# The first unit of weights multiplied for both tiles of tokens by row blocks, with its loads cut into pieces on two DMA queues

## The chip, the cores and the metric

The kernel runs on one core of a Trainium2 chip. The metric is the time of the whole launch on that core in microseconds: 2056.93 us is the median of three runs (2055.18 to 2057.09). Engines are named as the profile names them: PE (TensorE matmul) and PEld (its weight loads), DVE (VectorE), ACT (ScalarE), POOL (GpSimd), SP (SyncE, which here only issues DMAs). Each engine works through its own instructions in the order in which they were built.

## The reference, cut to what matters

A decoder trunk of four layers over 256 tokens of width 1024. Layer i is

```
x += 1/2 SwiGLU(rmsnorm x);  x += W_out [mixer heads | memory heads];  x += 1/2 SwiGLU(rmsnorm x)
swiglu(x) = (silu(x @ wg) * (x @ wu)) @ wd          # wg, wu: 1024 x 2816, wd: 2816 x 1024
rms_norm(x, g) = x * rsqrt(mean(x * x) + EPS) * g
```

with retention, indexed sparse attention, native sparse attention and again retention as the mixers of the four layers. Four heads of every layer attend to 256 memory tokens, which are normed by `rms_norm(mem)` first. All of it is float32. The change is in the first SwiGLU of the first layer: its first 256 gate and 256 up columns.

## The kernel before, in words

**Tiles and units.** The 256 tokens are two tiles of 128 (t = 0 and 1, `X[0]` and `X[1]`, 128 x 1024 each). All weights are streamed once, as units: a unit of kind "g" is 1024 rows x 512 columns (256 gate, 256 up), stored as two halves (`raw`, 128 x 2048 each, 1 MB; four row blocks of 128 rows each). There are three `raw` buffers. Both tiles use a unit before the next one comes.

**Products in three parts.** A float32 product is made of three matmuls (`mm3`, L231 to L235): high part x high part, high x low, low x high. So every quarter of a unit (two row blocks, 128 x 1024) is split: `hi` on ACT (L205) and `lo` = raw - hi on DVE (L206). The activations are split too: `norm_half` (L319) transposes four 128 x 128 blocks of `X` on PE (L329, into the bank `pT`), and makes `sh` on ACT (L333) and `sl` on DVE (L334), a block at a time, with the gain of the norm. A unit for one tile is 8 row blocks x 3 = 24 matmuls (`project`, L237) into one PSUM bank `pg`, of which there are two.

**What follows a unit.** For a unit of kind "g", ACT makes `th` (tanh, L1072), DVE `th` again (L1073) and `h` (L1075), which empties the bank; PE transposes `h` (L1081). `rh` and `r2` in these come from the token's norm: ACT squares a whole tile of `X` (`scr`, L341), and POOL makes `rstd_m`, `rstd`, `rh`, `r` of the sum (L314, L316, L344, L346).

**The memory's tokens.** `memory()` (L1178) loads two blocks `memx` of 512 KB on POOL's queue (L1184), and ACT squares them (L1186). On POOL these loads stand behind the norm of the first tile.

**The order.** The program is written by generators, one chain for each tile (`chain`, L1111) and one for the memory; a `tick` (L251) issues the steps that are due, one or two splits, and steps of a joint queue, whose number in a tick follows from a count of ticks (`JRATE`). A scheduler then fixes the order of each engine's instructions. At the start `run` (L1140) loads the identity, `X[0]` and the gains, then unit 0 in four pieces of 512 KB, then `X[1]` and unit 1, all on SP's queue; the constants `cf`, `cb`, `mqk` are written further down, on POOL's queue. Nine matmuls on zeros (`warm`) run on PE meanwhile.

## Time and profile before

| | |
|---|---|
| launch, median of 3 runs | 2056.93 us |
| span of the profiled execution, first to last instruction | 2052.0 us |
| median minus span (what lies around the span) | 4.9 us |
| PE busy | 2034.5 us, 99% of the span |
| PEld busy | 1652.5 us, 81% |
| DVE busy | 1257.3 us, 61% |
| ACT busy | 1025.5 us, 50% |
| POOL busy | 165.6 us, 8% |
| HBM read | 349.07 MB, 171 GB/s over the span |

A line of the timeline begins with the start and the length of an instruction (or of a run of like ones, xN) in us from the start of the span; what stands in brackets is the time the engine was idle before it, and what ended that. Neighbouring instructions of an engine overlap a little in the record, so the step from one start to the next is what an instruction costs in a queue; the length is what the last one of a chain costs. "Granted clock" is PEclk in tenths or hundredths of full speed: 1.00 is 2.4 GHz, 0.50 is 1.2 GHz.

### The profile page before, as it was taken

How to read it: one execution, taken by the hardware profiler on the slowest of the kernel's cores; microseconds unless marked ns; L12 is line 12 of the kernel's file. 1: busy time of each engine (PE TensorE's matmuls, PEld its weight loads, DVE VectorE, ACT ScalarE, POOL GpSimd, SP SyncE). 2: the span in 40 equal slices, each digit the busy share in tenths (PEclk: the TensorE clock that was granted, in tenths of full speed). 3: DMA queues.
4: the chain of work that ended last, by engine and by line, in shares of the span. 5: the costliest groups of instructions: out<-in, count | busy, mean ns of one | idle time of the engine just before them, and what ended most of it. 6: DMA issues, size and time to landing. Idle time of an engine off the chain costs nothing.

```text
span 2052.0 us, 25183 instructions
## 1 busy us (share of the span) xinstructions
PE 2034.5 (99%) x9658; PEld 1652.5 (81%) x9658; DVE 1257.3 (61%) x1996; ACT 1025.5 (50%) x1581; POOL 165.6 (8%) x290
## 2 busy tenths in 40 slices
PE   9999999999999999999999999999999999999999
PEld 6888777888888887888888878878888888778887
DVE  6555756555655687755665576665656656657553
ACT  6445555444544555544544455554445444546442
POOL 1000411000000122000000013220000000300000
PEclk9999999999999999999999999999999999999999
DMA  8454525445445423545445453134545545435452
GB/s 301 182 191 164 198 109 205 180 180 195 179 170 202 164 99 123 205 164 205 173 176 205 169 178 134 63 133 176 205 164 185 198 172 204 146 122 187 183 190 77
DMA packets 50153, 351.75 MB, mean 171 GB/s; under 512 B 5648, under 2 KB 5936, under 8 KB 9200
## 3 DMA queue, kind: packets, MB, share of 16 engines
q1 hardware_dynamic: 48816, 347.15, 46.3%
q0 software_dynamic: 640, 1.94, 0.3%
q8 instruction: 76, 1.25, 0.2%
q10 hardware_dynamic: 576, 1.05, 0.1%
q14 instruction: 45, 0.37, 0.1%
HBM read 349.07 MB, written 1.05 MB: 171 GB/s over the span
## 4 chain that ended last, share of the span: by engine, by line
PE 96%; DVE 2%; POOL 1%; ACT 1%; issue 0%; DMA 0%; SPq 0%; ACTq 0%; DVEq 0%; POOLq 0%
PE pg L235 16%; PE pg L233 16%; PE pg L234 16%; PE acc L233 8%; PE acc L234 8%; PE acc L235 8%; PE p L233 3%; PE p L235 3%; PE p L234 3%; PE pT L1081 2%; PE po L233 1%; PE po L234 1%; PE po L235 1%; PE pT L379 1%; PE pT L329 1%; PE nsa_s L429 1%
## 5 line engine op out<-in xcount | busy, mean ns | idle before, releaser
L206 DVE TENSOR_TENSOR lo<-raw,hi 128x1024 fp32r<-128x1024 f32 (+2 forms) x648 | 780.1, 1220 | 368.6 <-ACT hi L205 353.2
L205 ACT ACTIVATE hi<-raw 128x1024 fp32r<-128x1024 f32 (+2 forms) x648 | 667.3, 1049 | 373.0 <-PE acc L235 208.6
L233 PE MATMUL pg<-hi,sh 128*128 128x512 f32 x1408 | 563.2, 400 | 3.4 <-ACT hi L205 3.4
L235 PE MATMUL pg<-hi,sl 128*128 128x512 f32 x1408 | 552.0, 392 | 0.0
L234 PE MATMUL pg<-lo,sh 128*128 128x512 f32 x1408 | 550.1, 391 | 0.5 <-DVE lo L206 0.5
L235 PEld LDWEIGHTS pg<-hi,sl 128*128 128x128 f32 x1408 | 264.7, 188 | 57.6 <-DVE sl L334 0.3
L233 PEld LDWEIGHTS pg<-hi,sh 128*128 128x128 f32 x1408 | 265.0, 188 | 54.5 <-ACT hi L205 3.6
L234 PEld LDWEIGHTS pg<-lo,sh 128*128 128x128 f32 x1408 | 265.5, 189 | 52.8 <-DVE lo L206 1.0
L233 PE MATMUL acc<-hi,hT 128*128 128x512 f32 x704 | 281.2, 399 | 0.0
L234 PE MATMUL acc<-lo,hT 128*128 128x512 f32 x704 | 279.2, 397 | 0.0
L235 PE MATMUL acc<-hi,hT 128*128 128x512 f32 x704 | 277.5, 394 | 0.0
L1072 ACT ACTIVATE th<-pg,rh 128x256 f32<-128x256 f32 x176 | 83.6, 475 | 262.3 <-PE pg L235 262.3
L1073 DVE SCALAR_TENSOR_TENSOR th<-th,pg 128x256 f32<-128x256 f32 x176 | 73.5, 418 | 194.1 <-ACT th L1072 194.1
L235 PEld LDWEIGHTS acc<-hi,hT 128*128 128x128 f32 x704 | 132.3, 188 | 30.5 <-DVE hT L1083 0.2
L233 PEld LDWEIGHTS acc<-hi,hT 128*128 128x128 f32 x704 | 132.3, 188 | 30.1 <-ACT hT L1082 1.2
L234 PEld LDWEIGHTS acc<-lo,hT 128*128 128x128 f32 x704 | 132.5, 188 | 28.1
L1082 ACT ACTIVATE hT<-pT 128x256 fp32r<-128x256 f32 x176 | 65.9, 374 | 131.9 <-PE pT L1081 131.9
L233 PE MATMUL p<-hi,sh 128*128 128x512 f32 (+4 forms) x320 | 125.4, 392 | 0.0
L235 PE MATMUL p<-hi,sl 128*128 128x512 f32 (+4 forms) x320 | 120.9, 378 | 0.0
L234 PE MATMUL p<-lo,sh 128*128 128x512 f32 (+4 forms) x320 | 120.8, 377 | 0.0
L1083 DVE TENSOR_TENSOR hT<-pT,hT 128x256 fp32r<-128x256 f32 x176 | 74.1, 421 | 37.3 <-ACT hT L1082 37.2
L333 ACT ACTIVATE sh<-pT,gains 128x128 fp32r<-128x128 f32 x192 | 63.5, 364 | 59.1 <-PE pT L329 39.6
(287 smaller groups left out, 1793.1 us busy)
## 6 DMA issues: line engine op xcount, KB each, us to landing
raw<-gu SPq DMA_DIRECT2D x174, 1024.0 KB, 4.8
raw<-dn SPq DMA_DIRECT2D x88, 1024.0 KB, 4.8
raw<-ret SPq DMA_DIRECT2D x20, 1024.0 KB, 4.8
raw<-wout SPq DMA_DIRECT2D x16, 1024.0 KB, 4.8
raw<-mkv SPq DMA_DIRECT2D x8, 1024.0 KB, 4.9
raw<-nsa SPq DMA_DIRECT2D x6, 1024.0 KB, 4.8
raw<-memT SPq DMA_DIRECT2D x4, 1024.0 KB, 4.8
raw<-dsa SPq DMA_DIRECT2D x4, 768.0 KB, 4.3
```

The source lines that it names most:

```text
L205: nc.scalar.activation(hi, src, AF.Copy)
L206: nc.vector.tensor_sub(lo, src, hi.bitcast(F32))
L233: mm(out, ah, bh, start=start, stop=False)
L234: mm(out, ah, bl, start=False, stop=False)
L235: mm(out, al, bh, start=False, stop=stop)
L329: nc.tensor.transpose(p[:, k], self.X[t][:, c * 128:(c + 1) * 128], self.ident)
L333: nc.scalar.activation(hi[:, c], p[:, k], AF.Copy, scale=gain)
L1072: nc.scalar.activation(th, p[:, :256], AF.Tanh, scale=rh)
L1073: nc.vector.scalar_tensor_tensor(th, th, 1.0, p[:, :256], op0=OP.add, op1=OP.mult)
L1081: nc.tensor.transpose(c[:, k], h[:, k * 128:k * 128 + 128], self.ident)
L1082: nc.scalar.activation(hl[:, 0], c[:, :2], AF.Copy)
L1083: nc.vector.tensor_sub(hl[:, 1], c[:, :2], hl[:, 0].bitcast(F32))
```

## The change

Unit 0 is no longer taken by `project`. A new function `opening` loads, splits and multiplies it for both tiles, and returns the two banks, which `ffn` then uses. The loads of `X` and of unit 0's first half become pieces of 256 KB, those of its second half pieces of 512 KB; `ident`, `gains` and three of the four pieces of `X` go out on ACT's queue. Three of the four half-norms are made by `norm_wide`, with instructions of 512 columns. The squares for the norm's factors (`norm_stats`) are written after the matmuls of unit 0. Four more matmuls on zeros stand before the first real one. The call that loads the constants is written behind the sixth step of the main loop. Comments and docstrings go as well, which moves the line numbers.

```diff
+    def norm_wide(self, t, g, b, st):
+        hi, lo = st["s"]
+        p = self.pC("pT")
+        c = slice(4 * b, 4 * b + 4)
+        for k in range(4):
+            nc.tensor.transpose(p[:, k], self.X[t][:, (4 * b + k) * 128:(4 * b + k + 1) * 128], self.ident)
+        w = self.t2([128, 4, 128], "xg")
+        nc.vector.tensor_mul(w, p, self.gains[:, g, c, None].to_broadcast([128, 4, 128]))
+        nc.scalar.activation(hi[:, c], w, AF.Copy)
+        nc.vector.tensor_sub(lo[:, c], w, hi[:, c].bitcast(F32))
...
             if kind == "g":
-                p = self.pB("pg")
-                self.project(p, s, u)
+                if u == 0:
+                    p = self.first[t]
+                else:
+                    p = self.pB("pg")
+                    self.project(p, s, u)
...
+    def opening(self):
...
+        nc.sync.dma_start(self.X[0][:, col(0)], x[0:128, col(0)])
+        nc.scalar.dma_start(self.ident, a["ident"])
+        nc.sync.dma_start(raw[0][:, col(0)], w[0][:, col(0)])
+        nc.scalar.dma_start(self.gains.rearrange("p a b -> p (a b)"), a["gains"])
+        nc.scalar.dma_start(self.X[1][:, col(0)], x[128:256, col(0)])
+        nc.sync.dma_start(raw[0][:, col(1)], w[0][:, col(1)])
+        nc.scalar.dma_start(self.X[0][:, col(1)], x[0:128, col(1)])
+        nc.sync.dma_start(raw[0][:, col(2)], w[0][:, col(2)])
+        nc.scalar.dma_start(self.X[1][:, col(1)], x[128:256, col(1)])
+        nc.sync.dma_start(raw[0][:, col(3)], w[0][:, col(3)])
+        for b in range(2):
+            c = slice(1024 * b, 1024 * b + 1024)
+            nc.sync.dma_start(raw[1][:, c], w[1][:, c])
+        self.fetch()
...
+        self.norm_half(0, g, 0, self.st[0])
+        halve(0, 1)
+        self.idle(4)
+        multiply(0, 0)
...
+        self.norm_wide(1, g, 0, self.st[1])
+        halve(1, 1)
+        multiply(0, 1)
+        multiply(1, 0)
+        multiply(1, 1)
+        self.norm_wide(0, g, 1, self.st[0])
+        halve(2, 1)
+        multiply(0, 2)
+        multiply(1, 2)
+        self.norm_wide(1, g, 1, self.st[1])
+        halve(3, 1)
+        multiply(0, 3)
+        multiply(1, 3)
+        for k in (4, 6):
+            halve(k, 2)
+            for t, j in ((0, 0), (1, 0), (0, 1), (1, 1)):
+                multiply(t, k + j)
+        for t in range(2):
+            self.norm_stats(t, self.st[t])
+        return p
...
-        for b in range(2):
-            self.norm_half(t, 2 * self.layers[0], b, st)
-        if t:
-            for x in range(2):
-                self.norm_stats(x, self.st[x])
...
-        nc.gpsimd.dma_start(self.cf, a["cf"])
-        nc.gpsimd.dma_start(self.cb, a["cb"])
...
+            if n == 5:
+                constants_in()
```

`halve(k, n)` is the split of n row blocks from the k-th (L1163 on ACT, L1164 on DVE), `multiply(t, k)` the three matmuls of row block k for tile t.

Three places show how the engines' orders move. The first is ACT, around the first `th`. Before, with the norm's blocks (L333), the splits of unit 1 (L205), `th` of tile 0 (L1072) and the squares of the memory's tokens (L1186):

```order
L205 ACTIVATE hi<-raw 128x1024 [waits DMAHW0_49]
L333 ACTIVATE sh_148<-pT,gains 128x128 [waits DVE_49] x2
L205 ACTIVATE hi<-raw 128x1024
L1072 ACTIVATE th<-pg,rh 128x256 [waits PE_49,Pool_49]
L333 ACTIVATE sh_148<-pT,gains 128x128 [waits DVE_49] x2
L205 ACTIVATE hi<-raw 128x1024 [waits DMAHW1_49]
L205 ACTIVATE hi<-raw 128x1024
L1186 ACTIVATE memx,memss<-memx 128x1024 [waits DMASW3_49]
L1186 ACTIVATE memx,memss<-memx 128x1024 [waits DMASW4_49]
L1082 ACTIVATE hT<-pT 128x256 [waits PE_49]
```

And in the changed kernel (L1163 splits unit 0, L349 squares `X`, L200 splits unit 1, L1252 squares `memx`, L1083 is `th`):

```order
L1163 ACTIVATE hi<-raw 128x1024 [waits DMAHW3_49]
L349 ACTIVATE scr,ss<-x_70 128x1024 [waits DMAHW6_49]
L342 ACTIVATE sh_136<-xg 128x512 [waits DVE_49]
L349 ACTIVATE scr,ss<-x_71 128x1024 [waits DMAHW4_49,DMAHW0_49]
L200 ACTIVATE hi<-raw 128x1024 [waits DMAHW4_49]
L200 ACTIVATE hi<-raw 128x1024
L1252 ACTIVATE memx,memss<-memx 128x1024 [waits DMASW3_49]
L200 ACTIVATE hi<-raw 128x1024 [waits DMAHW5_49]
L1083 ACTIVATE th<-pg,rh 128x256 [waits PE_49,Pool_49]
L200 ACTIVATE hi<-raw 128x1024
L1252 ACTIVATE memx,memss<-memx 128x1024 [waits DMASW4_49]
```

The square of `X[0]`, the second instruction of ACT before, now stands behind the splits of unit 0, and the first `th` behind a square of `memx`, which waits for its load.

The second place is PE, where unit 0 ends and unit 1 begins. Before (sh_148 and sl_149 are tile 1's operand, sh_104 tile 0's; L1081 transposes `h` of tile 0):

```order
L235 MATMUL pg<-hi,sl_149 128x512
L233 MATMUL pg<-hi,sh_148 128x512 [waits Activation_49]
L1081 MATMUL pT<-ident,h 128x128 [waits DVE_49]
L1081 MATMUL pT<-ident,h 128x128
L234 MATMUL pg<-lo,sh_148 128x512
L235 MATMUL pg<-hi,sl_149 128x512
L233 MATMUL pg<-hi,sh_104 128x512 [waits PE_49]
```

And changed (sh_110 is tile 0's operand, sh_136 tile 1's; L1092 transposes `h`):

```order
L230 MATMUL pg<-hi,sl_111 128x512
L228 MATMUL pg<-hi,sh_136 128x512
L229 MATMUL pg<-lo,sh_136 128x512
L230 MATMUL pg<-hi,sl_137 128x512
L1092 MATMUL pT<-ident,h 128x128 [waits DVE_49]
L1092 MATMUL pT<-ident,h 128x128
L228 MATMUL pg<-hi,sh_110 128x512 [waits PE_49,Activation_49]
```

The transposes of tile 0's `h` stood 22 matmuls behind tile 0's last matmul, and now stand three behind it, ahead of all of unit 1.

The third is POOL, in the changed kernel, from its first DMA (L1240 to L1242 are the constants, L1250 the memory's tokens):

```order
L1240 DMA cf<-cf 128x657
L1241 DMA cb<-cb 128x542
L1242 DMA mqk<-mqk 128x8
L1246 ISA
L1246 TENSOR_TENSOR mqkp<-mqk 128x4 [waits DMASW2_49]
L309 TENSOR_SCALAR rstd_m<-ss 128x1 [waits Activation_49]
L311 TENSOR_TENSOR rstd<-rstd_m,neghalf 128x1 [waits DVE_49,Pool_49]
L352 TENSOR_SCALAR rh<-rstd 128x1 [waits Pool_49]
L354 TENSOR_TENSOR r_235<-rstd 128x1
L1250 DMA memx<-mem 128x1024
L309 TENSOR_SCALAR rstd_m<-ss 128x1 [waits Activation_49]
L1250 DMA memx<-mem 128x1024
```

Here nothing moved: before, the same twelve stand in the same order with the same waits, the constants first. Elsewhere the orders differ only in the native sparse attention of the third layer, where steps of the two tiles stand a few rows earlier or later, since two ticks fewer were counted.

## Rows read from the trace of the kernel before

**Rows 1.** The page, busy time of each engine in the whole span.

```profile
PE 2034.5 (99%) x9658; PEld 1652.5 (81%) x9658; DVE 1257.3 (61%) x1996; ACT 1025.5 (50%) x1581; POOL 165.6 (8%) x290
```

**Rows 2.** Busy time by stretches of the opening: stretch, its length, then busy us (and instructions) of PE, PEld, DVE, ACT, POOL, then granted clock, DMA share, GB/s.

```profile
0.00:5.00 5.00, 3.82 (x10) 1.23 (x10) 0.29 (x2) 1.41 (x2) 2.06 (x7) 1.00 0.56 186
5.00:10.00 5.00, 1.63 (x10) 1.39 (x9) 0.83 (x3) 2.98 (x7) 0.92 (x3) 0.94 1.01 332
10.00:15.00 5.00, 4.54 (x10) 3.25 (x11) 5.00 (x10) 5.00 (x10) 1.82 (x4) 0.50 1.03 424
15.00:20.00 5.00, 5.00 (x25) 4.11 (x25) 3.35 (x6) 3.64 (x10) 2.27 (x5) 0.88 1.01 417
20.00:25.00 5.00, 5.00 (x23) 3.87 (x22) 5.00 (x10) 5.00 (x9) 0.57 (x1) 1.00 0.90 346
25.00:30.00 5.00, 5.00 (x25) 4.16 (x24) 4.20 (x7) 4.89 (x8) 1.86 (x4) 1.00 0.88 308
```

**Rows 3.** PE in the timeline of the opening: the first transposes, the first two matmuls, two more of unit 0 that follow each other, the transposes of tile 0's `h`, the matmul behind them, and the first matmul of unit 1 (25.62).

```profile
5.00 1.53 PE L329 MATMUL pT<-ident,x 128*128 128x128 f32 x8
9.89 0.79 PE L233 MATMUL pg<-hi,sh 128*128 128x512 f32 x1 [3.37 <-ACT hi L205]
11.15 0.80 PE L234 MATMUL pg<-lo,sh 128*128 128x512 f32 x1 [0.47 <-DVE lo L206]
13.02 0.63 PE L235 MATMUL pg<-hi,sl 128*128 128x512 f32 x1
13.45 0.63 PE L233 MATMUL pg<-hi,sh 128*128 128x512 f32 x1
24.94 0.38 PE L1081 MATMUL pT<-ident,h 128*128 128x128 f32 x2
25.07 0.48 PE L234 MATMUL pg<-lo,sh 128*128 128x512 f32 x1
25.62 0.40 PE L233 MATMUL pg<-hi,sh 128*128 128x512 f32 x1
```

**Rows 4.** Stretches of 0.2 us around the fall and the rise of the granted clock (columns as in rows 2).

```profile
9.20:9.40 0.20, 0.00 (x0) 0.00 (x0) 0.00 (x0) 0.20 (x1) 0.18 (x1) 0.96 0.90 369
9.40:9.60 0.20, 0.00 (x0) 0.00 (x0) 0.00 (x0) 0.20 (x1) 0.13 (x1) 0.50 0.98 389
16.20:16.40 0.20, 0.20 (x4) 0.20 (x3) 0.00 (x0) 0.00 (x0) 0.20 (x1) 0.97 1.60 655
```

**Rows 5.** ACT in the timeline of the opening.

```profile
4.87 1.06 ACT L341 ACTIVATE scr<-x 128x1024 f32<-128x1024 f32 x1 [2.86 <-DMA x<-x]
8.78 1.06 ACT L205 ACTIVATE hi<-raw 128x1024 fp32r<-128x1024 f32 x1 [1.85 <-DMA raw<-gu]
14.14 1.07 ACT L341 ACTIVATE scr<-x 128x1024 f32<-128x1024 f32 x1
15.09 0.22 ACT L341 ACTIVATION_READ_ACCUMULATOR scr<-x 128x1 f32 x1
20.42 0.48 ACT L1072 ACTIVATE th<-pg,rh 128x256 f32<-128x256 f32 x1
20.78 0.64 ACT L333 ACTIVATE sh<-pT,gains 128x128 fp32r<-128x128 f32 x2
23.17 1.08 ACT L1186 ACTIVATE memx<-memx 128x1024 f32<-128x1024 f32 x1
24.21 1.08 ACT L1186 ACTIVATE memx<-memx 128x1024 f32<-128x1024 f32 x1
26.94 2.96 ACT L205 ACTIVATE hi<-raw 128x1024 fp32r<-128x1024 f32 x3
```

**Rows 6.** DVE in the same timeline: splits (L206), blocks of the norm (L334), `h`; and a line of 128x512 from the end of the kernel.

```profile
9.87 1.22 DVE L206 TENSOR_TENSOR lo<-raw,hi 128x1024 fp32r<-128x1024 f32 x1 [2.56 <-ACT hi L205]
11.01 0.60 DVE L334 SCALAR_TENSOR_TENSOR sl<-pT,gains,sh 128x128 fp32r<-128x128 f32 x2
22.75 1.22 DVE L206 TENSOR_TENSOR lo<-raw,hi 128x1024 fp32r<-128x1024 f32 x1
23.89 0.47 DVE L1075 SCALAR_TENSOR_TENSOR h<-th,r,pg 128x256 f32<-128x256 f32 x1
2042.75 0.69 DVE L1100 SCALAR_TENSOR_TENSOR x<-acc,x 128x512 f32<-128x512 f32 x1 [2.10 <-PE acc L235]
```

**Rows 7.** POOL in the same timeline: the norm of tile 0, and the first load of the memory's tokens.

```profile
9.19 0.19 POOL L314 TENSOR_SCALAR rstd_m<-ss 128x1 f32<-128x1 f32 x1
11.29 0.62 POOL L1184 DMA_DIRECT2D memx<-mem  x1
```

**Rows 8.** DMA issues, KB each and us from issue to landing: the two loads of `memx` (issued at 11.29 and 16.16), the constants `cf`, and `X[1]` (issued at 4.13), each from the stretch in which it ran.

```profile
memx<-mem POOLq DMA_DIRECT2D x1, 512.0 KB, 7.8
memx<-mem POOLq DMA_DIRECT2D x1, 512.0 KB, 7.6
cf<-cf POOLq DMA_DIRECT2D x1, 328.5 KB, 4.6
x<-x SPq DMA_DIRECT2D x1, 512.0 KB, 9.6
```

**Rows 9.** Two stretches of the third layer's native sparse attention (columns as in rows 2).

```profile
1240.00:1300.00 60.00, 58.93 (x387) 51.25 (x385) 35.32 (x88) 30.89 (x65) 16.11 (x25) 1.00 0.32 116
1300.00:1350.00 50.00, 49.59 (x311) 39.77 (x311) 33.25 (x83) 27.64 (x56) 15.71 (x21) 1.00 0.28 105
```

More of the change, by code (lines that the diff above doesn't have):

```diff
@@ L181, in fetch @@
             r = self.wp.tile([128, n], F32, name="raw", tag="raw", bufs=3)
-            if u == 0:
-                for b in range(2):
-                    c = slice(b * n // 2, (b + 1) * n // 2)
-                    self.nc.sync.dma_start(r[:, c], ap[:, c])
-            else:
-                self.nc.sync.dma_start(r, ap)
+            self.nc.sync.dma_start(r, ap)
             self.raw[u].append(r)
@@ L335, in norm_half @@
                                            op0=OP.mult, op1=OP.subtract)
+    def norm_wide(self, t, g, b, st):
+        nc = self.nc
+        hi, lo = st["s"]
[7 more added lines that the diff above has]
+        nc.vector.tensor_sub(lo[:, c], w, hi[:, c].bitcast(F32))
     def norm_stats(self, t, st):
@@ L1109, in ffn, with idle, halve, multiply @@
             self.norm_stats(t, st)
+    def idle(self, n):
+        for _ in range(n):
+            self.nc.tensor.matmul(self.pw, self.warm[:, :128], self.warm, start=True, stop=True)
+    def opening(self):
+        nc, a, g = self.nc, self.a, 2 * self.layers[0]
+        x, w = a["x"], self.units[0][1]
+        self.n_fetch = self.n_split = 1
+        raw = [self.wp.tile([128, 2048], F32, name="raw", tag="raw", bufs=3) for _ in range(2)]
+        col = lambda k: slice(512 * k, 512 * k + 512)
+        nc.sync.dma_start(self.X[0][:, col(0)], x[0:128, col(0)])
[12 more added lines that the diff above has]
+        self.fetch()
+        self.warm = self.cp.tile([128, 512], BF, name="warm")
+        nc.vector.memset(self.warm, 0.0)
+        nc.vector.memset(self.neghalf, -0.5)
+        self.pw = self.bank("pw", "A")
+        self.idle(WARM)
+        p = [self.pB("pg") for _ in range(2)]
+        hi, lo = {}, {}
+        def halve(k, n):
+            if k % 2 == 0:
+                hi[k // 2] = self.wp.tile([128, 1024], F32R, name="hi", tag="hi", bufs=HALVES)
+                lo[k // 2] = self.wp.tile([128, 1024], F32R, name="lo", tag="lo", bufs=HALVES)
+            src = raw[k // 4][:, k % 4 * 512:(k % 4 + n) * 512]
+            c = slice(k % 2 * 512, (k % 2 + n) * 512)
+            nc.scalar.activation(hi[k // 2][:, c], src, AF.Copy)
+            nc.vector.tensor_sub(lo[k // 2][:, c], src, hi[k // 2][:, c].bitcast(F32))
+        def multiply(t, k):
+            s = self.st[t]["s"]
+            self.mm3(p[t], s[0][:, k], s[1][:, k], hi[k // 2][:, col(k % 2)], lo[k // 2][:, col(k % 2)],
+                     k == 0, k == 7)
+        self.norm_half(0, g, 0, self.st[0])
+        halve(0, 1)
+        self.idle(4)
+        multiply(0, 0)
+        self.st[1]["s"] = tuple(self.ap.tile([128, 8, 128], F32R, name=f"{n}1", bufs=1) for n in ("sh", "sl"))
+        self.norm_wide(1, g, 0, self.st[1])
[18 more added lines that the diff above has]
+        return p
@@ L1114, in chain @@
         st = self.st[t]
-        for b in range(2):
-            self.norm_half(t, 2 * self.layers[0], b, st)
-        if t:
-            for x in range(2):
-                self.norm_stats(x, self.st[x])
         for i in self.layers:
@@ L1148, in run, with constants_in @@
         self.neghalf = cp.tile([128, 12], F32, name="neghalf")
-        nc.sync.dma_start(self.ident, a["ident"])
-        nc.sync.dma_start(self.X[0], a["x"][0:128])
-        nc.sync.dma_start(self.gains.rearrange("p a b -> p (a b)"), a["gains"])
-        warm = cp.tile([128, 512], BF, name="warm")
-        nc.vector.memset(warm, 0.0)
-        nc.vector.memset(self.neghalf, -0.5)
-        pw = self.pB("pw")
-        for _ in range(WARM):
-            nc.tensor.matmul(pw, warm[:, :128], warm, start=True, stop=True)
-        self.fetch()
-        nc.sync.dma_start(self.X[1], a["x"][128:])
-        self.fetch()
+        self.first = self.opening()
         chains = [self.chain(0), self.chain(1), self.mem_chain()]
-        next(chains[0])
+        for c in chains:
+            next(c)
         self.split()
-        self.split_some(4)
-        next(chains[1])
-        next(chains[2])
-        self.split_some(0, 0)
-        self.split()
-        nc.gpsimd.dma_start(self.cf, a["cf"])
-        nc.gpsimd.dma_start(self.cb, a["cb"])
         self.fetch()
         mq = cp.tile([128, 2, 4], F32, name="mqk")
-        nc.gpsimd.dma_start(mq.rearrange("p a b -> p (a b)"), a["mqk"])
-        late = []
+        def constants_in():
+            nc.gpsimd.dma_start(self.cf, a["cf"])
+            nc.gpsimd.dma_start(self.cb, a["cb"])
+            nc.gpsimd.dma_start(mq.rearrange("p a b -> p (a b)"), a["mqk"])
         def memory():
```

## The prediction

> **What bounds the kernel now.** The page comes first: PE is busy 2034.5 of 2052.0 us [rows 1], so the whole kernel is one chain of matmuls, and a change can only win where PE stands still or runs slowly. The stretches of the opening show where that is [rows 2]: from 5 to 10 us PE is busy 1.63 of 5 us, from 10 to 15 it is busy but at half clock (0.50), and from 20 us on it is full at 1.00. The timeline of PE gives the mark that I measure by: the first matmul of unit 1 starts at 25.62 us, with tile 0's `h` already transposed [rows 3]. Behind that mark the order of work is the same in both kernels up to the third layer, and PE is full; so what the change does to this mark it does to the end, except for the clock and for the third layer.
>
> What the 25.62 us hold: the first piece of weights lands at 8.78 and ACT splits it at once [rows 5], DVE's `lo` starts at 9.87 [rows 6], PE's first matmul at 9.89 after 3.37 us of idleness [rows 3]. Around 9.4, 2.9 us after the last transpose ended, the granted clock fell to 0.50, and it rose at 16.2 [rows 4]. Matmuls of 512 columns step by 0.43 us at the low level (13.02 to 13.45 [rows 3]) and by 0.22 to 0.23 at the high one (23 in the 5 us from 20 [rows 2]). The 48 matmuls of unit 0 therefore took from 9.89 to 25.62 us where 48 x 0.23 = 11 would do: some 4.7 us is what this opening could give at most, if it went as it is meant to.
>
> **The change, part by part.** *Smaller pieces.* The engines that move data are full from 5 us on (share 1.01, 1.03, 1.01 [rows 2]), so cutting the loads changes who lands first, not when all have landed. Before, the first 512 KB of weights landed at 8.78 behind 640 KB of other loads. Now the first 256 KB lie behind or beside 256 of `X[0]`, `ident`, `gains` and part of `X[1]`; in proportion that is about 7.2 us, 1.6 us earlier. The last piece of unit 0 is now the last of exactly the loads that before ended with `X[1]` (ident, gains, both tiles, unit 0): that landed at 4.13 + 9.6 = 13.7 [rows 8], and I put the last piece there. Low bound 12.9: the 328 KB of `cf` shared the early engines, and 328 KB at 0.42 MB per us are 0.8 us, if the second queue pushes them back. High bound 15.2, if rows of 2 KB move as slowly as the loads did between 5 and 10 us (332 against 424 GB/s).
>
> *Constants later.* They don't move: POOL has nothing in front of them, and its order before and after is the same. Nothing gained.
>
> *Splits and norms.* On DVE, 16 blocks of `sl` (0.30 us each by the pair at 11.01) become four, plus three `xg` and three `sl` of 512 columns at about 0.61 (0.69 less the overlap [rows 6]): 4.8 against 4.9 us. On ACT the same count saves some 1.5 us. Both are hidden behind the loads until 13.7 us, so I cost them at nothing; if the loads come early, DVE's work decides (second rival).
>
> *Squares and `memx`.* This is the term that decides. Before, ACT squared `X[0]` at 4.87, as its first work, POOL made the norm's factors from 9.19, and the load of `memx` went out at 11.29, 2.1 us behind [rows 5, 7]. It landed 7.8 us later, at 19.1, well ahead of its square at 23.17; the second took 7.6 [rows 8]. Now the square of `X[0]` stands behind all splits of unit 0, POOL still makes the factors first, and on ACT the square of `memx` stands in front of the third quarter of unit 1, of tile 0's first `th` and of the last quarter. So ACT waits for this load, and behind it everything that PE needs next: PE has tile 0's transposes three matmuls behind unit 0's end, in front of all of unit 1.
>
> The chain, by steps from one start to the next: last piece of unit 0 lands 13.7; its split, 0.95 (three in 2.96 with a last one of 1.06 [rows 5]), 14.65; square and its read-out, 14.14 to 15.31 = 1.17, at 15.8; POOL's factors 2.1, so the load goes out at 17.9; landing 7.7, at 25.6; square of `memx` 1.04 (23.17 to 24.21), 26.65; third quarter 0.95, 27.6; `th` 0.36 (20.42 to 20.78), 27.95; last quarter 1.06, 29.0; its `lo` on DVE 1.14 (22.75 to 23.89), 30.15; `h` 0.47, 30.6; two transposes 0.13 (24.94 to 25.07), 30.75. Unit 1 starts at about 30.8 instead of 25.6: **+5.2 us**. ACT reaches the square of `memx` at about 19.5 (15.8 + 0.5 + 1.17 + two quarters of 0.95), so it would stand idle for six. PE ends unit 0 near 21 to 26, by its clock; it isn't late.
>
> For the landing I have 4.6 us (`cf`, 328 KB, beside SP's loads) as the low end and 7.8 as the high one. I take 7.7, since both loads of `memx` showed it, the second in the same company that it has now: the second half of unit 1 and the first of unit 2 on SP's queue.
>
> By the Trainium skill (DMA: Bandwidth & Descriptors, Queues, rings and completion order) each DMA engine takes turns between the queues that have work for it, a packet at a time. By that rule alone POOL's 512 KB would get half of the roughly 420 GB/s and land in some 4.5 us (an estimate from that page's rule, with its 2 us of fixed cost), the mark would stand at 27.6, and the loss would be about 3 us less. The trace doesn't agree: beside SP's queue POOL's loads of this size took 7.6 and 7.8.
>
> *The clock.* If PE stands still from about 23 to 30.6, that is longer than the idle stretch (3.37 us by its row) within which the grant fell to 0.50. When matmuls had begun again without gaps at 11.15 [rows 3], it took 5 us until 16.2 for the grant to rise [rows 4]. Five us at half speed lose 2.5: **+2.5 us**. Low end 0 (short wait), high end 3.1 (from 9.89 to 16.2).
>
> *The second `memx`* goes out about 1 us behind the first and may land some us later; it holds tile 1's `th`, which PE needs 12 matmuls into unit 1 (2.8 us, or 5.2 at half clock). I cost it at nothing because of that cover; without it, up to 2 us.
>
> *Third layer.* Steps of the joint queue fall into other places. PE was idle only 1.07 and 0.41 us in the two stretches shown [rows 9], so I take nothing, with ends of -2 and +2.
>
> *Four matmuls on zeros* run while PE has no data: nothing.
>
> **Sum.** 5.2 + 2.5 = 7.7 us on the profiled execution: 2052.0 + 4.9 around the span (which is the median, 2056.9) + 7.7 = **2064.6 us**.
>
> **Rivals.** *First: the load of `memx` comes sooner* (4.6 us, like `cf`): it lands at 22.5, the mark is 27.7 by the same steps, +2.1, and PE idles between 2 and 5 us, so the clock costs 0 to 2.5: 2059 to 2061.5, say 2060.5. For it: SP has fewer loads outstanding at 18 us than at 11. Against it: the row of 7.6. This is also where the rule of the page would put it.
>
> *Second, on the other side: the opening wins.* `memx` lands before ACT has come to it (within 1.6 us of its issue, or the issue comes 4 us earlier), and the mark is DVE's backlog: first `lo` at 7.8, then ten instructions of 512 columns (6.1), four blocks (1.2), six quarters (6.8), `th` and `h` (0.8), 22.7 with a start of unit 1 at 22.9: -2.7, 2054.2. What speaks for it is the idle PE and the half clock up to 15 us [rows 2]; against it, every landing row of `memx`. It decides only if the load's square finds its data by about 19.5.
>
> *Third: PE at half clock through the opening.* Matmuls begin near 8.5 with gaps, which may hold the grant at 0.50: 48 x 0.43 = 20.6, end at 29.1, then the last quarter, `lo` and `h` behind `th` (0.36 + 1.06 + 1.14 + 0.47): 32.3 at the mark, +6.7, with an idle stretch of three us behind it: 2063.6 to 2066.1. It lies within the forecast's range and only gives it another cause.
>
> *Fourth: it moves nothing.* The gain of 1.6 us at the first piece and a shorter wait for `memx` (landing at 20.5) cancel: 2057. For it speaks that unit 1's last quarters land no earlier than before.
>
> **How the numbers follow.** Forecast 0.55 (own range 2061.5 to 2068: landing 6 to 7.8, clock 2.5 to 3.1, last piece 12.9 to 15.2); first rival 0.20; third 0.08; second 0.08; fourth 0.09. A measurement of this kernel tells from no change about 0.2%, 4.1 us: below 2052.8 is faster, above 2061.0 slower. Slower: forecast and third and a quarter of the first less the forecast's low tail, 0.61. Faster: the second rival's 2054.2 stays inside the 0.2%, so it needs the third layer's -2 as well or loads faster than any row shows: 0.06. Same: the rest, 0.33. The range that leaves out two in ten goes from 2055.5, which cuts the second rival, to 2068.5.
>
> **What would show it.** ACT idle for several us in front of the square of `memx`, with that load as releaser; PE waiting for `h` at the transposes, and unit 1 starting near 30.8; the granted clock at 0.50 behind that. I am wrong if ACT finds `memx` landed, if unit 1 starts before 25.6, if the constants go out later than 3 us, or if the difference arises in the third layer.

## The result, and the profile after

The changed kernel takes 2068.58 us (median of 4 runs, 2067.66 to 2072.63) against 2056.55 us (4 runs, 2055.18 to 2057.09) of the kernel before: ratio 1.0060, 95% interval 1.0048 to 1.0072. The forecast was 2064.6 us, with 2068.5 as the upper end of its range. It is slower by 12.0 us, where +7.7 had been forecast. The span of its profiled execution is 2066.3 us and its time 2068.02 us.

The page's row of busy times answers to [rows 1]:

```profile
PE 2037.5 (99%) x9662; PEld 1652.1 (80%) x9662; DVE 1259.8 (61%) x1992; ACT 1024.3 (50%) x1574; POOL 166.0 (8%) x290
```

The work is the same and PE's busy time has grown by 3.0 us only; the span has grown by 14.3, so most of it is PE standing still. The stretches of the opening, with the columns of [rows 2], show where:

```profile
10.00:15.00 5.00, 4.71 (x17) 3.37 (x18) 3.44 (x8) 3.99 (x9) 0.19 (x1) 0.66 1.04 415
15.00:20.00 5.00, 5.00 (x26) 4.14 (x25) 5.00 (x8) 5.00 (x9) 2.69 (x3) 1.00 0.36 120
20.00:25.00 5.00, 4.63 (x21) 3.51 (x19) 2.55 (x3) 0.52 (x1) 4.10 (x8) 1.00 0.97 380
25.00:30.00 5.00, 0.00 (x0) 0.00 (x0) 0.00 (x0) 0.93 (x1) 0.00 (x0) 0.85 0.94 383
30.00:35.00 5.00, 0.66 (x3) 0.66 (x4) 3.60 (x5) 4.82 (x9) 1.66 (x4) 0.50 0.11 14
35.00:40.00 5.00, 5.00 (x17) 3.91 (x16) 4.04 (x6) 3.39 (x5) 0.00 (x0) 0.62 0.67 236
```

From 25 to 30 us PE, PEld and DVE do nothing at all and the DMA engines are at 0.94: everything waits for a load. From 30 to 35 ACT (4.82 of 5 us) and DVE (3.60) work off what had waited, PE is busy for 0.66 us, and the granted clock is at 0.50. A second thing is new from 15 to 20 us: the DMA share is 0.36, where before it was 1.01. SP's load behind the one of 9.84 us goes out only at 17.48, after a `lo` of unit 0 (L1164) has freed a `raw` buffer; before, the one in its place went out at 12.77. The view of waits from 24 to 40 us (engine, line, what it waited for: total, times, longest) names the chain:

```profile
PE pT L1092 <- DVE h L1086: 9.7, 1, 9.7
DVE lo L201 <- ACT hi L200: 8.9, 2, 8.6
ACT memx L1252 <- DMA memx<-mem: 8.6, 1, 8.6
```

Read from the bottom: ACT waits for `memx`, DVE for ACT, PE for DVE. In the timeline of POOL, ACT and PE the same chain has its lengths; these lines answer to [rows 7], [rows 5] and [rows 3]:

```profile
17.14 0.32 POOL L309 TENSOR_SCALAR rstd_m<-ss 128x1 f32<-128x1 f32 x1 [6.74 <-ACT scr L349]
17.54 1.44 POOL L311 TENSOR_TENSOR rstd<-rstd_m,neghalf 128x1 f32<-128x1 f32 x1
19.07 1.30 POOL L352 TENSOR_SCALAR rh<-rstd 128x1 f32<-128x1 f32 x1
20.34 1.13 POOL L354 TENSOR_TENSOR r<-rstd 128x1 f32<-128x1 f32 x1
21.41 0.62 POOL L1250 DMA_DIRECT2D memx<-mem  x1
```

```profile
14.97 1.05 ACT L1163 ACTIVATE hi<-raw 128x1024 fp32r<-128x1024 f32 x1
15.92 1.04 ACT L349 ACTIVATE scr<-x 128x1024 f32<-128x1024 f32 x1
29.07 1.06 ACT L1252 ACTIVATE memx<-memx 128x1024 f32<-128x1024 f32 x1 [8.56 <-DMA memx<-mem]
31.07 0.45 ACT L1083 ACTIVATE th<-pg,rh 128x256 f32<-128x256 f32 x1
```

```profile
24.25 0.39 PE L230 MATMUL pg<-hi,sl 128*128 128x512 f32 x1
34.34 0.69 PE L1092 MATMUL pT<-ident,h 128*128 128x128 f32 x2 [9.70 <-DVE h L1086]
34.68 0.78 PE L228 MATMUL pg<-hi,sh 128*128 128x512 f32 x1
35.25 0.63 PE L229 MATMUL pg<-lo,sh 128*128 128x512 f32 x1
```

Unit 1 starts at 34.68 instead of 25.62 us, +9.06. Its first matmuls step by 0.43 us until 38.66, where the clock is back.

What the change was written for didn't come either. The first piece of weights is split at 5.63 us, yet the first matmul of unit 0 starts at 10.17, where before it started at 9.89 [rows 3]: on PE it stands behind transposes of `X[1]`, whose first piece landed only then.

```profile
9.87 0.55 PE L339 MATMUL pT<-ident,x 128*128 128x128 f32 x3 [3.59 <-DMA x<-x]
10.17 0.48 PE L228 MATMUL pg<-hi,sh 128*128 128x512 f32 x1
```

To follow the loss through the launch I compare the start of each `th` of ACT (176 in every kernel, in the same order) with the one in the trace of before. For the changed kernel the difference is 11.05 us at the fourth `th` (37 us), 11.91 at the one of 1184 us, 13.29 at the next but one (1386 us, so across the third layer), 14.11 at the last. So: 9.1 at the mark, 2.0 by the clock behind it, 1.4 in the third layer, and some 1.7 in small steps, none over 0.16 us, spread over the rest, whose cause I did not find.

In each profiled execution of these runs the time is 1.7 to 1.8 us above the span (here 2068.02 and 2066.3). By that the profiled execution of the kernel before took about 2053.8 us (2052.0 + 1.8), at the lower edge of all its timed runs (2053.73 to 2062.80). That is why the spans differ by 14.3 and the medians by 12.0.

### The profile page after: what moved, and what is told of

Same layout as the page of the kernel before. It is cut to its first block, busy times and chain, and to the rows that moved or that the text cites. A ratio compares the mean times of both kernels' runs of the same rounds, so it can differ in the third digit from the quotient of the medians.

```text
span 2066.3 us, 25188 instructions
## 1 busy us (share of the span) xinstructions
PE 2037.5 (99%) x9662; PEld 1652.1 (80%) x9662; DVE 1259.8 (61%) x1992; ACT 1024.3 (50%) x1574; POOL 166.0 (8%) x290
## 3 DMA queue, kind: packets, MB, share of 16 engines
q8 instruction: 76, 1.25, 0.2%
## 4 chain that ended last, share of the span: by engine, by line
PE 95%; DVE 2%; POOL 1%; issue 1%; ACT 1%; DMA 1%; ACTq 0%; DVEq 0%; POOLq 0%
PE pg L230 15%; PE pg L228 15%; PE pg L229 15%; PE acc L228 8%; PE acc L229 8%; PE acc L230 8%; PE p L228 3%; PE p L230 3%; PE p L229 3%; PE pT L1092 2%; PE pT L387 1%; PE po L228 1%; PE po L229 1%; PE po L230 1%; PE pT L324 1%
## 5 line engine op out<-in xcount | busy, mean ns | idle before, releaser
L200 ACT ACTIVATE hi<-raw 128x1024 fp32r<-128x1024 f32 (+2 forms) x644 | 663.1, 1049 | 369.7 <-PE acc L230 208.9
L1083 ACT ACTIVATE th<-pg,rh 128x256 f32<-128x256 f32 x176 | 83.7, 476 | 265.7 <-PE pg L230 265.7
L309 POOL TENSOR_SCALAR rstd_m<-ss 128x1 f32<-128x1 f32 x24 | 10.4, 435 | 1001.9 <-ACT scr L349 1001.8
```

The lines of the kernel that those rows point to most:

```text
L200: nc.scalar.activation(hi, src, AF.Copy)
L1083: nc.scalar.activation(th, p[:, :256], AF.Tanh, scale=rh)
```

## The experiments

All of them start from the changed kernel. This table has the mark (start of the first matmul of unit 1), the difference to the trace of the kernel before at three `th`, and the median time. The medians of the kernel before beside them were 2057.25, 2058.00, 2057.66 and 2057.53 us in the four groups of runs.

| kernel | mark | at 37 us | at 1184 | at 1386 | median us |
|---|---|---|---|---|---|
| before | 25.62 | 0 | 0 | 0 | 2057 |
| changed | 34.68 | 11.05 | 11.91 | 13.29 | 2068.58 |
| e1, memx loaded first | 30.47 | 4.95 | 5.66 | 6.92 | 2063.60 |
| e2, memx squared later | 27.13 | 4.47 | 4.16 | 5.41 | 2061.19 |
| e3, factors earlier | 27.91 | 4.78 | 5.57 | 8.45 | 2062.68 |
| e5, clock kept up | 36.46 | 11.24 | 11.93 | 13.26 | 2068.06 |
| e7, e2 + another bank | 23.89 | 3.12 | 4.14 | 5.45 | 2057.49 |
| e8, e2 + tail by tile | 23.38 | 0.39 | 0.45 | 1.82 | 2058.32 |
| e6, ticks as before | 35.22 | 11.63 | 12.31 | 15.24 | 2069.22 |
| e4, constants later | 33.29 | 10.14 | 10.79 | 13.65 | 2068.59 |
| e10, all together | 23.35 | 0.64 | 1.24 | 8.85 | 2060.18 |
| e13, one queue | 28.13 | 5.05 | 5.72 | 8.59 | 2063.38 |
| e14, e10 + memx behind weights | 22.98 | -2.53 | -2.67 | 0.27 | 2055.81 |

**e1: `memx` first.** Is it the load of `memx`?

```diff
+        memx = [self.t4([128, 1024], "memx") for _ in range(2)]
+        for m in range(2):
+            nc.gpsimd.dma_start(memx[m], a["mem"][m * 128:(m + 1) * 128])
...
-                x = self.t4([128, 1024], "memx")
-                nc.gpsimd.dma_start(x, a["mem"][m * 128:(m + 1) * 128])
+                x = memx[m]
```

> The changed kernel, but the two loads of memx are POOL's first DMAs, ahead of the constants; everything behind them is as it was. Theory (ACT's wait for the first memx, issued at 21.4 us behind the norm's factors, holds the third quarter, th, h and so all of unit 1): both squares find their data, the first matmul of unit 1 starts between 25 and 27 us instead of 34.68, PE isn't idle before it for more than 2 us, the granted clock stays at 1.00 there, and the time is 9 to 11 us less than the changed kernel's, 2057 to 2060. Rival (the loss comes from the row-block order of unit 0, one pg bank held by each tile, or from ACT's longer backlog; the load is only the last of several things that are late): the mark stays beyond 31 us and the time falls by less than 4 us. Second rival (the constants or early weights now land later by as much): the first matmul of unit 0 later than 11 us, time above 2063.

ACT no longer waits for `memx`, and the loss falls from 12 to 6.4 us (ratio to before 1.0038, 1.0021 to 1.0055). That is half of the theory's gain; the mark lies between the two theories. Two lines say why, one of ACT and one of PE:

```profile
12.71 0.63 ACT L1163 ACTIVATE hi<-raw 128x512 fp32r<-128x512 f32 x1 [2.24 <-DMA raw<-gu]
30.27 0.44 PE L1092 MATMUL pT<-ident,h 128*128 128x128 f32 x2 [2.54 <-DVE h L1086]
```

The megabyte in front pushed the weights back, as the second rival had it (the first matmul of unit 0 at 11.04, the time above 2063; the third piece is split at 12.71, in the changed kernel at 10.57), so unit 0 ended 3 us later; and at its end PE still waited 2.54 us for `h`, with nothing of `memx` in between. There is a second cause.

**e2: the load stays late, its square moves.**

```diff
+                if u == 0 and t == 1:
+                    self.one = self.cp.tile([128, 1], F32, name="one")
+                    nc.vector.tensor_scalar(self.one, h[:, :1], 0.0, 1.0, op0=OP.mult, op1=OP.add)
...
-                nc.scalar.activation(x, x, AF.Square, accum_out=ss)
+                nc.scalar.activation(x, x, AF.Square, scale=self.one, accum_out=ss)
```

> The changed kernel, with the loads of memx as late as there, but the squares of memx wait for the first h of tile 1 too (one more DVE instruction of 128x1, and a scale of 1.0), so that they stand on ACT behind th of both tiles. Theory (it is the place of the square on ACT, not the load's own lateness or its share of the DMA engines): the load still goes out at 20 to 22 us and lands near 29, yet unit 1 starts between 25 and 28 us and the time is 8 to 11 us less than the changed kernel's, 2057 to 2061. Rival (the late load itself delays what PE needs, by taking the DMA engines from the weights): unit 1 starts beyond 31 us, gain below 4 us.

The mark is 27.13, as the theory had it, with the load at 21.56 as late as ever: with the square out of `th`'s way 7.5 of the 9.06 us are gone, though the load is late, so its share of the DMA engines isn't what they came from. The loss takes both, the square in front of `th` and a load that is late: e3 and e13 below leave the square there, bring the load out earlier, and win back 6.8 and 6.5 us of the mark. The time fell by 7.4 us (ratio to before 1.0018, 1.0008 to 1.0028), a little less than expected. Behind the mark the trace loses 3.0 us more up to 37 us (1.51 to 4.47): the first matmuls step by 0.43 us there too, and PE waits 1.26 us in front of the transposes at 38.76. What is left at the mark:

```profile
22.42 1.06 ACT L200 ACTIVATE hi<-raw 128x1024 fp32r<-128x1024 f32 x1 [1.76 <-DMA raw<-gu]
23.67 0.47 ACT L1083 ACTIVATE th<-pg,rh 128x256 f32<-128x256 f32 x1 [0.19 <-PE pg L230]
26.26 0.47 DVE L1086 SCALAR_TENSOR_TENSOR h<-th,r,pg 128x256 f32<-128x256 f32 x1
26.79 0.69 PE L1095 MATMUL pT<-ident,h 128*128 128x128 f32 x2 [2.54 <-DVE h L1086]
```

`th` could not start before 23.67, because tile 0's last matmul of unit 0 now stands three matmuls before the end of all; `h` follows 2.6 us later behind two splits on DVE; and PE has nothing else to do, since both `pg` banks are still held.

**e3: the factors earlier.** `norm_stats(0, ...)` is written behind tile 0's second half-norm and `norm_stats(1, ...)` behind tile 1's, instead of both at the end of `opening`.

> The changed kernel, but the squares and factors of each tile's norm are written right after that tile's second half-norm, so the square of X[0] comes about 5 us earlier on ACT; the loads of memx stay behind the first factors on POOL. The squares of memx both stand before the first th on ACT. Theory (each us by which the factors are earlier is a us of the mark, until ACT's own backlog decides): the load of the first memx goes out at 14 to 17 us, lands at 22 to 25, unit 1 starts at 27 to 31 us, time 4 to 9 us less than the changed kernel's, 2060 to 2065. If instead the second memx, the loads' time under more traffic (over 9 us) or the clock decides, the mark stays above 32 and the time above 2066.

As expected: the load goes out at 13.68, the mark is 27.91, the time 2062.68 (ratio to before 1.0026, 1.0015 to 1.0036). ACT finds `memx` landed; PE waits 3.40 us for `h`, as in e2. The four instructions of the factors took 1.4 us here (12.29 to 13.68), not 4.3.

**e7 and e8: the cover.** Two ways to give PE work while `h` is made, both on top of e2. e7 puts tile 1's sum into another bank, so that unit 1 finds one free; e8 writes the tail of unit 0 tile by tile, so that tile 1's matmuls stand behind tile 0's.

```diff
-        p = [self.pB("pg") for _ in range(2)]
+        p = [self.pB("pg"), self.bank("pw", "A")]
```

```diff
-        for k in (4, 6):
-            halve(k, 2)
-            for t, j in ((0, 0), (1, 0), (0, 1), (1, 1)):
-                multiply(t, k + j)
+        halve(4, 2)
+        halve(6, 2)
+        for t in range(2):
+            for k in range(4, 8):
+                multiply(t, k)
```

> The kernel of e2 (squares of memx behind both th), but tile 1's sum of unit 0 is kept in a bank of the other group, so that unit 1 finds a free bank. New theory, formed after e2 still showed 2.5 us of idle PE and a mark at 27.13: the row-block order keeps both pg banks to the end of unit 0, so unit 1 must wait until th, two splits and h of tile 0 are done, which tile 1's 24 matmuls covered before. Then unit 1 starts within 0.5 us of the end of unit 0, at 24 to 24.6 us, at a clock of 1.00, and the time is 3.5 to 5 us less than e2's: 2056 to 2058. Rival (unit 1's quarters, not the bank, are what PE waits for; the third was split only at 22.42 to 24.65 in e2): the mark comes early but PE stops inside unit 1 for as long, time within 1.5 us of e2's 2061.2.

> The kernel of e2, with the last four row blocks of unit 0 written tile by tile (all of tile 0, then all of tile 1) instead of alternating. By the theory that tile 1's matmuls must cover tile 0's th and h, nine matmuls instead of three are the cover, 1.4 us more: unit 1 starts 1 to 1.6 us earlier than e2's 27.13, at 25.5 to 26.2, PE's idle time before the transposes falls from 2.54 to about 1.2 us, time 2059 to 2060.5. By the rival (unit 1's quarters decide) nothing changes, 2061 to 2062.

In both PE goes from unit 0 into unit 1 without a gap, and the marks are 23.89 and 23.38, earlier than before the change: the missing cover is shown. Both then stop inside the following work, in front of the transposes of a later `h`; first e7, then e8:

```profile
35.94 0.41 PE L1095 MATMUL pT<-ident,h 128*128 128x128 f32 x2 [2.96 <-DVE h L1086]
```

```profile
35.22 0.41 PE L1095 MATMUL pT<-ident,h 128*128 128x128 f32 x2 [1.75 <-DVE h L1086]
```

So for e7 the rival was half right, the early mark was given back at 35.94: at 37 us its trace is only 1.35 us ahead of e2's. The medians fell more, by 3.7 us, as the theory had it. e8 keeps what it gained on e2 (3.75 us at the mark, 4.08 at 37 us), but not its lead on before: 2.24 us ahead at the mark, 0.39 behind at 37 us. In front of its stop ACT had waited 2.28 us for `memx` at 29.77, ahead of a `th` of unit 1. At the mark it gained more than expected: ACT and DVE now take `th` and `h` ahead of unit 1's later splits (`th` at 21.24). Ratios to before: 0.9992 (0.9983 to 1.0001) and 1.0002 (0.9992 to 1.0012).

**e12: what holds POOL.** In the changed kernel the factors took 4.27 us, before 2.1. A probe of 60 instructions of one element, which add work and change no result:

```diff
+        pr = self.cp.tile([128, 60], F32, name="probe")
+        for i in range(60):
+            nc.gpsimd.tensor_scalar(pr[:, i:i + 1], self.neghalf[:, :1], 0.5, None, op0=OP.mult)
```

> The changed kernel with 60 more POOL instructions of one element per row (128x1, from a constant into a scratch tile that nothing reads) right behind the first load of the constants, so that they run beside all that DVE does from 3 us on; cb and mqk go out behind them. Theory (POOL is held while DVE runs an instruction with two operands in SBUF): each takes 0.18 to 0.25 us while DVE is idle, and 0.6 to 1.3 us where it starts beside a lo (two operands in SBUF); the time itself says nothing and may be some us above the changed kernel's. Rival (POOL's factors in the changed kernel were slow for another reason, as waits for semaphores or the kind of operation): all 60 take 0.18 to 0.25 us.

Its one run took 2067.55 us. 57 took 0.20 to 0.26 us; three took 0.65 to 0.74, and just three DVE instructions with both operands in SBUF stand beside the 60. Here is POOL in the timeline beside a `lo` (6.53), beside nothing (x11 is a run of eleven), beside `xg`, which reads one operand from PSUM (x6), and beside `sl<-xg` (12.72); `lo` and `sl<-xg` read both operands from SBUF. Behind it the DVE instructions beside them:

```profile
6.53 0.74 POOL L1154 TENSOR_SCALAR probe<-neghalf 128x1 f32<-128x1 f32 x1
7.40 1.88 POOL L1154 TENSOR_SCALAR probe<-neghalf 128x1 f32<-128x1 f32 x11
9.25 1.04 POOL L1154 TENSOR_SCALAR probe<-neghalf 128x1 f32<-128x1 f32 x6
12.72 0.73 POOL L1154 TENSOR_SCALAR probe<-neghalf 128x1 f32<-128x1 f32 x1
```

```profile
6.51 0.69 DVE L1167 TENSOR_TENSOR lo<-raw,hi 128x512 fp32r<-128x512 f32 x1 [5.37 <-ACT hi L1166]
9.44 0.69 DVE L341 TENSOR_TENSOR xg<-pT,gains 128x512 f32<-128x512 f32 x1 [1.97 <-PE pT L339]
12.69 0.69 DVE L343 TENSOR_TENSOR sl<-xg,sh 128x512 fp32r<-128x512 f32 x1
```

The two slow ones shown began 0.02 to 0.03 us behind the start of such a DVE instruction and ended 0.07 behind its end (7.27 and 7.20; 13.45 and 13.38); beside `xg` six in a row take 0.17 us each. In the changed kernel it is the same with longer instructions: `rh` ends at 20.37 and `lo` (19.06, 1.22 us) at 20.28; `r` ends at 21.47 and the next `lo` (20.20, 1.22 us) at 21.42. `rstd`, which takes 0.57 us where nothing holds it (e3), starts beside a `lo` that ends at 18.55 and ends 0.43 behind it, at 18.98. The Trainium skill states this as a rule (SBUF — State Buffer, Who interferes with whom: a DVE instruction with two SBUF inputs contends with a GpSimd instruction that reads SBUF). The trace agrees.

**e4 and e13: the loads.** e4 issues `cf` and `cb` on SP's queue (`nc.sync` for `nc.gpsimd` in `constants_in`), where they really go out later; e13 issues all loads of `opening` on SP's queue (`nc.sync` for `nc.scalar`).

> The changed kernel with the constants cf and cb (600 KB) issued on SP's queue behind the first half of unit 1, so that they really are later; mqk alone stays POOL's first load. Theory (600 KB beside the first loads cost 600 KB / 0.42 MB per us = 1.4 us of the loads' time): X[1]'s first piece lands 0.7 to 1.4 us earlier than 9.8 us, the last split of unit 0 begins at 13.6 to 14.4 instead of 14.97, the load of memx goes out 0.6 to 1.4 us earlier than 21.41, the mark moves by the same from 34.68, time 2066.5 to 2068. Rival (the early loads are held by their own queues, not by the constants): no start moves by more than 0.3 us.

> The changed kernel with all loads of the opening on SP's queue, in the same order in which they are written. Theory (the two queues decide who lands first, not when all have landed, and the mark hangs on the last piece): X[1]'s first piece lands by 8.5 instead of 9.8 us, but the split of the last piece of unit 0 begins within 0.7 us of 14.97, the mark within 1 us of 34.68, time 2067 to 2070. Rival (issue of ten loads in a row on one queue, or turns between queues, hold the loads): that split moves by more than 1 us, and the mark and the time with it.

e4 did in the trace what was expected, or a little more: the last split of unit 0 at 13.47, the load of `memx` out at 19.84, the mark 1.39 us earlier. (`cf` and `cb` are 328.5 and 135.5 KB, 464 KB and not the 600 of the text on record; at 0.42 MB per us that is 1.1 us.) The time didn't show it (2068.59): its trace gains 2.86 us of loss across the third layer, the changed kernel's 1.38, with the clock at 0.91 in 1340 to 1360. e13 came out otherwise than both theories said: the last split of unit 0 was later (16.49), yet the mark came 6.5 us earlier and the time 5.2 us down (2063.38, ratio to before 1.0028, 1.0018 to 1.0038). The queues had changed ACT's order: with `X[0]`'s second piece ahead, the square of `X[0]` stood at 10.10 again, and POOL's factors took 2.0 us (11.34 to 13.35). The timeline, and the DMA issues (KB each and us to landing):

```profile
10.10 1.06 ACT L349 ACTIVATE scr<-x 128x1024 f32<-128x1024 f32 x1 [0.18 <-DMA x<-x]
13.35 0.62 POOL L1250 DMA_DIRECT2D memx<-mem  x1
```

```profile
memx<-mem POOLq DMA_DIRECT2D x2, 512.0 KB, 4.8
```

So the square was late for two reasons, the place where `norm_stats` is written and the second queue; undoing either one (e3, e13) brings the load of `memx` out by 13.7 us.

**e5: the clock's share.** 36 more matmuls, which add work to PE and change no result, behind unit 0.

```diff
+        s = self.st[1]["s"]
+        for _ in range(36):
+            self.nc.tensor.matmul(self.pw, s[1][:, 7], hi[3][:, col(1)], start=True, stop=True)
```

> The changed kernel with 36 more matmuls of 128x512 (into the scratch bank of the zeros; no result depends on them) behind the last matmul of unit 0, to keep PE busy for 8.2 of the 9.7 us in which it waits. Theory of the clock's share: the granted clock stays at 1.00 through the mark, the matmuls from the mark on step by 0.23 instead of 0.43 us, the mark stays at 34 to 35.5, and the time falls by 1.5 to 2.5 us, to 2066 to 2067. Rival (the half clock behind the mark costs nothing, since unit 1's quarters or tile 1's h are late anyway): no change within 0.7 us, PE idle for some 2 us behind the mark instead.

```profile
26.00 8.32 PE L1197 MATMUL pw<-hi,sl 128*128 128x512 f32 x36
36.27 0.44 PE L1092 MATMUL pT<-ident,h 128*128 128x128 f32 x2 [1.95 <-DVE h L1086]
```

The clock stayed at 1.00 and the steps behind the mark at 0.23 us, but `memx` took 9.05 us to land this time (21.95 to 31.00), and the mark came 1.78 us later. The time fell by 0.5 us, not by 1.5 to 2.5. Since a mark later by 1.78 left the difference at 37 us at 11.24, against 11.05, the full clock was worth some 1.6 us; by the total alone this run shows nothing.

**e6: the third layer.** `self.ticks` begins at 2 instead of 0; the order of the third layer is then that of before.

> The changed kernel with the count of ticks begun at 2, which gives the third layer the order that it had before and touches nothing else. Theory (the growth of the difference by 1.45 us inside the third layer comes from the two ticks that are no longer counted): the difference to the kernel before is the same on both sides of the third layer within 0.3 us, and the time falls by 1.2 to 1.6 us, to 2067.0 to 2067.4. Rival (the growth comes of the later start, through buffers and loads, not of the order): it stays, time 2068.3 to 2068.9.

By the totals this failed: 2069.22 us, and the difference grows by 2.93 across the third layer. The stretches tell it apart, with the columns of [rows 9]; first the changed kernel, then e6:

```profile
1240.00:1300.00 60.00, 57.65 (x357) 48.43 (x357) 36.95 (x87) 29.35 (x59) 18.08 (x25) 1.00 0.33 114
```

```profile
1240.00:1300.00 60.00, 58.93 (x362) 49.57 (x360) 38.26 (x90) 28.76 (x58) 18.76 (x25) 1.00 0.34 115
...
1346.00:1348.00 2.00, 2.00 (x15) 1.83 (x14) 0.90 (x2) 1.15 (x2) 0.00 (x0) 0.68 0.00 0
1348.00:1350.00 2.00, 2.00 (x10) 1.96 (x10) 1.18 (x6) 0.00 (x0) 0.00 (x0) 0.50 0.34 57
```

With the order of before, PE is busy 58.93 of 60 us again, as in [rows 9]; in the changed order it is idle 1.28 us more. So the ticks cost some 1.3 us, and the difference grows by 1.25 to 1.38 us in every profile of the table that has the changed order and no half clock in the third layer (changed, e1, e2, e5, e7, e8). What came on top in e6 is a stretch at half clock from 1346 us on, with PE's rows busy all the time. Stretches of 20 us with a mean clock of 0.74 to 0.91 stand in the third layer in six profiles (e3, e4, e6, e13, e14 and, at two places, e10), and in none of the other eight. No run here explains them. In e6 the clock fell during or right behind sixteen matmuls of 65 columns (from 1345.04, with twelve of 15 columns behind them); such matmuls stand in the profiles without a fall too (in the changed kernel at 1346.63 and 1348.14). The kernel before has no such stretch in its profile, but its runs differ in the mean granted clock, and the longer ones have the lower clock: beside e10, the two at 0.994 took 2061.09 and 2061.71 us, the six at 0.998 2054.87 to 2057.94.

**e10 and e14: all together.** e10 is e8 with the square of `memx` behind tile 1's `h` of unit 1 (`if u == 1 and t == 1`), `cf` and `cb` as in e4, and the ticks as in e6. e14 adds the loads of `memx` on SP's queue, where they stand behind nine more loads of 1 MB of weights. It also writes the call that loads the constants behind the eleventh step of the main loop instead of the sixth, which the text on record doesn't say; `cf` and `cb` keep their place in SP's queue and go out at 9.17 and 9.72 (in e10 at 8.25 and 9.97).

> All that the runs so far showed, together: the changed kernel with the squares of memx behind tile 1's h of unit 1, the tail of unit 0 tile by tile, cf and cb on SP behind the first half of unit 1, and the count of ticks begun at 2. Theory (mark held by memx on ACT, by the uncovered h, by the loads that the constants push back, and third layer by the ticks): unit 1 starts at 21.5 to 23.2 us instead of 25.62, PE isn't idle for more than 0.7 us at one place between there and 45 us, the lead over the profile of the kernel before is 2 to 4 us and the same on both sides of the third layer within 0.3, where no stretch of half clock lies in between; time 2052 to 2055.5, ratio 0.9975 to 0.9992. Rival (the next limit, the loads of unit 2 behind the free buffers, or the clock, takes it back): lead below 1 us at 45 us, time 2056 to 2058.

> The kernel of e10 with the two loads of memx on SP's queue too, behind the loads of the first seven units, so that nothing but weights moves while units 1 and 2 are loaded. Theory (in e10 the opening's lead was given back at 35.38, where PE waited 2.62 us for h, whose th stood on ACT behind the splits of unit 2, whose first half landed only at 30.93 beside 1 MB of memx; 1 MB at 0.42 MB per us are 2.4 us): that half lands at 28 to 29.5, PE isn't idle for more than 0.7 us between 23 and 45 us, the difference to the profile of the kernel before is -2 to -3 us at 45 us. The time follows if no half clock comes: 2054 to 2057, ratio 0.997 to 1.000. Rival (the loads wait for free buffers, not for the DMA engines): the half lands after 30 as in e10 and PE waits for about 2 us, difference above -1 us, time 2057 to 2060.

e10 reached its mark (23.35) and lost the lead again, as its rival said, and in its trace half clock at two places of the third layer cost another 7.6 us. It took 2060.18 us (ratio 1.0014, 1.0003 to 1.0024). One line of ACT and one of PE:

```profile
30.93 2.01 ACT L200 ACTIVATE hi<-raw 128x1024 fp32r<-128x1024 f32 x2 [3.47 <-DMA raw<-gu]
35.38 0.41 PE L1095 MATMUL pT<-ident,h 128*128 128x128 f32 x2 [2.62 <-DVE h L1086]
```

`th` of unit 1 stands behind that split and waited for the weights with it (it is the second half of unit 2; the text on record for e14 calls it the first). With `memx` out of the way, e14 splits that half at 26.99 without a wait, and PE has no gap between 23 and 45 us:

```profile
20.00:40.00 20.00, 20.00 (x93) 16.34 (x92) 18.84 (x26) 14.08 (x19) 2.34 (x5) 1.00 0.91 340
1320.00:1340.00 20.00, 20.00 (x110) 16.62 (x109) 9.89 (x28) 11.16 (x19) 5.02 (x7) 0.83 0.16 54
```

It runs 2.5 to 2.7 us ahead of the trace of before for 1150 us, and then loses 2.9 of it in a stretch at clock 0.83. Its time is 2055.81 us (12 runs, 2051.69 to 2062.38) against 2057.53: ratio 0.9994 (0.9984 to 1.0005). It is clearly faster than the changed kernel; that it is faster than the kernel before is not shown.

## Why the prediction was wrong, point by point

The mechanism was right: ACT idle in front of the square of `memx` with that load as releaser (forecast six us, measured 8.56), PE waiting for `h` at the transposes, unit 1 late, half clock behind it. The size was off, and the steps say where.

- *"POOL's factors 2.1, so the load goes out at 17.9"* is the step that failed. They took 4.27 us (17.14 to 21.41), each of the four beside a `lo` that holds it (e12 shows how): **+2.2**. The prediction took the sum of the four from [rows 7], from a place where DVE ran one `lo` beside them, and moved it to a place where DVE runs `lo` after `lo`. Taken one by one, the rows of before held the warning: `rh`, one element, beside the `lo` that starts at 9.87 [rows 6].

```profile
10.12 1.06 POOL L344 TENSOR_SCALAR rh<-rstd 128x1 f32<-128x1 f32 x1
```

- *"Square and its read-out, at 15.8"*: it ended at 17.05, **+1.2**. The length (1.17) was right. The last piece landed at 14.4 (issued at 6.09, 8.3 us to landing), 0.7 later than the 13.7 that I had taken, and ACT began its split at 14.97, behind a block of the norm (14.45, 0.62 us) that I had left out. e4, without the constants in front, has this split at 13.47.
- *Landing 7.7*: 7.66 by the starts in the timeline (21.41 to 29.07). The first rival, 4.6 us, was wrong here. Yet the two loads landed in 4.7 and 3.8 us in e3 and in 5.0 and 4.6 in e13, and in 7.1 to 12.3 in the other runs that issue them on POOL's queue (12.3 in e2); so that the size came out to 0.04 us was partly luck. What decides I did not find out: the DMA engines were full (share 1.00 from 13.4 to 18 us) in e13 too. (By the rule of turns between queues in the Trainium skill, DMA: Bandwidth & Descriptors, Queues, rings and completion order, the prediction's estimate was 4.5: e3 and e13 are near it, the changed kernel is not.)
- *The rest of the chain, 5.15*: 5.61, **+0.45**. Together 1.2 + 2.2 + 0.45 = 3.85, which is what the mark has over the forecast (9.06 against 5.2). With 1.4 in the third layer and 1.7 in small steps, less 0.5 of the clock, that is 6.45 of the 6.6 us by which the span missed (14.3 against 7.7); the medians missed by 4.3.
- *The clock, +2.5*: 2.0 by the trace of the changed kernel; e5's trace gives some 1.6.
- *Third layer, nothing*: +1.3 to 1.4, inside the ends of -2 and +2 that I had named. e6 shows that it is the ticks.
- *Constants don't move; pieces, splits, zeros nothing*: the constants did go out first. e4 shows that they cost 1.4 us at the mark, which loading them later, as the change's code is written to, would have saved. The early pieces gained nothing: PE's first matmul came at 10.17, where the third rival had taken 8.5.
- *4.9 us around the span*: it is 1.8. The other 3.1 were a profiled execution faster than the median. The forecast was built on the difference and on the median, so this did no harm to it; it does explain 2.3 us between spans and medians.
- *Second rival, 22.9 if `memx` landed early*: e1 to e3 found `memx` landed, or moved its square, and stood at 27 to 30. That rival let `h` follow DVE's backlog alone; the splits of unit 1 waited for weights until 22.42 (e2), behind a stretch from 15 to 20 us in which the DMA engines were at 0.30, and PE had no cover. I had written that tile 0's transposes now stand three matmuls behind unit 0's end, and gave it no price of its own: 2.5 to 3.4 us (e2, e3).
- *Third rival, half clock through the opening*: not so. The granted clock was 0.66 from 10 to 15 us and 1.00 from 15 to 20, and unit 0 ended at 24.64, not 29.1.

## What to carry to other kernels

When a step is moved, take its duration from rows beside the same neighbours as at its new place, not from where it ran before: POOL's four tiny instructions cost 1.4, 2.1 or 4.3 us by what DVE did beside them. An instruction that waits for a load holds everything that stands behind it on its engine: before work is moved to a later place, look at what will then wait behind it. And two sums that share the banks should not end together; whichever ends first needs the other's matmuls as a cover (e7, e8: 3 to 4 us at the mark).
